# Beginning and end of the MLP of a two-layer encoder trunk: the order of up blocks, Strassen combinations, transposes and weight splits

## The chip, the cores and the metric

The kernel runs on one core of a Trainium2 chip. The time is that of one execution on the device in microseconds (us); of several runs the median is taken. Engines are named as in the profile: PE is TensorE (matrix products and transposes), DVE is VectorE, ACT is ScalarE, POOL is GpSimd, SP is SyncE, which issues the transfers from HBM.

## What is computed

The reference is a trunk of two layers on 512 tokens with 1024 features, in float32. Each layer has a mixer (dilated window attention in layer 0, latent attention in layer 1), a squared-ReLU MLP and a gated input embedding; the change lies in the last two and at their seams:

```
x = x + sq_relu_mlp(rmsnorm(x, mlp_norm[i]), w_up[i], w_down[i])
gate = jax.nn.sigmoid(rmsnorm(x, ple_norm[i]) @ w_ple_gate[i])
x = x + gate * (p[i] @ w_ple_proj[i])
...
def sq_relu_mlp(h, w_up, w_down):
    return jnp.square(jax.nn.relu(h @ w_up)) @ w_down
```

`w_up` is 1024 x 4096, `w_down` 4096 x 1024. The root mean square of `rmsnorm` runs over the 1024 features of a token.

## The kernel before, in words

**Products in three parts.** Every float32 matrix product is made of three products in a reduced type: each operand is split into a rounded high part and the low rest, and `mm3` (lines 219 to 221) adds high x high, low x high (or the mirrored pair) and high x low in one PSUM bank. A weight block of 128 x 1024 comes by DMA into a tile `wr`, ScalarE casts it to the high part `wh` (line 191), VectorE subtracts to get the low part `wl` (line 192). These three tags have three buffers each. Operands made in the kernel are split the same way by `split` (lines 226, 227, with a gain 229, 230) into `unit` tiles `u` of 128 x 1024, of which there are 24; there are 18 `half` tiles `h` of 128 x 512 and 8 PSUM banks `ps`.

**The order of weights** is a list made ahead (`_mlp_blocks`); `load` fetches a block and up to `ahead` (2) of its successors in that list, so its order sets SP's queue. The order of instructions on each engine is settled by a scheduler when the kernel is built, from the order in which the program asks for them; an engine then runs its own list in order and waits for others by semaphores.

**The MLP** (`mlp`, lines 699 to 856) runs over 4 chunks of 1024 hidden features. A chunk has 8 up blocks (`up`: `dense` products into a bank, `relu` on VectorE in line 728, the square on ScalarE in line 730, then the splits of the operands). From the fourth up block on `left` (lines 755 to 765) makes sums and differences of the operand's quarters. The product with `w_down` is a Strassen form with seven products, `prod(c, p)` for p = 1 to 7, each in two halves b = 0, 1 of 12 matrix products; its weights are quarters of `w_down` or their combinations. For these, `quarters` (line 148) issues three loads of 256 KB for each k = 0 to 3 into `half` tiles, and `combine` (lines 153 to 155) makes three differences of each on VectorE. Products share accumulating pairs of banks: P1, P6, P7, P4 follow each other in one pair, P5 and P3 in another, and behind a product `put` adds the banks to `acc` in SBUF (line 719) or copies them (line 722). The seven products of chunk c are interleaved with the up blocks of chunk c + 1; the first chunk's up blocks run ahead of the loop. In layer 0 they begin with `first`, four blocks whose products lie beside the attention's end, then up block 4, the norm's column sums (`columns`: products with ones in line 314, then `rsqrt`, a chain of 13 small VectorE steps in lines 246 to 259) and `row`, which spreads the result over partitions by PE transposes (line 267) and multiplies it in at each `relu`.

**The end of the MLP.** In the last chunk the products run in the order `LAST`; `embed` (lines 858 to 869) makes the embedding's projection of four blocks behind P6 and P7. `turned(m)` transposes a 128-feature block of `acc` back (four PE transposes, line 781), adds it to the residual x (line 341), splits it for the gate's products (lines 229, 230) and squares it for the gate's norm `nG` (ScalarE in lines 288 and 291; the sum of squares in line 292 on `eng`, GpSimd by default, the last of the eight on VectorE). Four of the eight `turned` stand behind P5, ahead of P3, four behind P3. Then `gate` (layer 0) or, in layer 1, a last stage with token halves runs its products with the norm's chain beside gate block 0.

## Time and profile before

| | |
|---|---|
| median of 3 runs | 1255.61 us (1255.6 to 1255.73) |
| the profiled execution's own time | 1254.16 us |
| its span on the core | 1252.3 us |
| mean granted PE clock | 0.991 of full speed |
| PE busy | 1215.8 us, 97% |
| VectorE busy | 972.4 us, 78% |
| ScalarE busy | 673.4 us, 54% |
| GpSimd busy | 136.4 us, 11% |

The profile records one execution: the span runs from the first instruction to the last, and the execution's own time holds 1.9 us around it. Busy time is the time in which an engine works on an instruction; a wait in the timeline stands in brackets in front of the instruction that waited, with the instruction that released it. The granted clock is given as a share of full speed; half speed is the lower of its two levels.

### The profile page before, as it was taken

The numbers are of one execution on the slowest core, as the hardware profiler recorded it, in microseconds if no ns is written. First come the engines' busy times: TensorE is split into PE (matmuls) and PEld (weight loads), VectorE is DVE, ScalarE is ACT, GpSimd is POOL, SyncE is SP. The second block draws the span as 40 slices with busy tenths as digits, with TensorE's granted clock in tenths as the row PEclk, the third lists the DMA queues.
The fourth block names the chain that finished last, engine by engine and source line by source line (L and its number), as shares of the span: only waits on it lengthen the run. The fifth ranks groups of instructions, "written<-read, shape, count | busy, mean of one in ns | idle before, by whom it ended". The sixth has DMA issues, their size and how long they took to land.

```text
span 1252.3 us, 16676 instructions
## 1 busy us (share of the span) xinstructions
PE 1215.8 (97%) x6096; PEld 1028.0 (82%) x6096; DVE 972.4 (78%) x1610; ACT 673.4 (54%) x1111; POOL 136.4 (11%) x177
## 2 busy tenths in 40 slices
PE   8999999999999999999989999999999999999996
PEld 6888878877888888887879888888888888888796
DVE  6566666788777877788878998968777778778877
ACT  5466564564354443555558887754545435435553
POOL 5000000000000000003234443220000000000300
PEclk9999999999999999999999999999999999999998
DMA  6222113263533534422211010126244354343242
GB/s 214 83 68 68 59 51 110 97 214 118 185 126 110 170 123 130 140 101 89 81 51 38 20 49 18 52 84 227 101 150 158 113 185 132 101 142 113 93 152 102
DMA packets 48178, 138.39 MB, mean 111 GB/s; under 512 B 5600, under 2 KB 6368, under 8 KB 48096
## 3 DMA queue, kind: packets, MB, share of 16 engines
q1 hardware_dynamic: 48096, 137.32, 33.2%
q8 instruction: 48, 0.79, 0.3%
q14 instruction: 34, 0.28, 0.1%
HBM read 135.21 MB, written 2.10 MB: 110 GB/s over the span
## 4 chain that ended last, share of the span: by engine, by line
PE 85%; DVE 8%; ACT 5%; issue 1%; DMA 0%; DVEq 0%; SPq 0%; ACTq 0%
PE ps L219 26%; PE ps L221 26%; PE ps L220 26%; PE ps L1057 2%; DVE wl L192 1%; DVE u L227 1%; PE ps L1079 1%; PE ps L1073 1%; DVE u L230 1%; ACT wh L191 1%; ACT u L226 1%; ACT h L226 1%; DVE x L341 1%; ACT qk L440 0%; PE ps L314 0%
## 5 line engine op out<-in xcount | busy, mean ns | idle before, releaser
L191 ACT CAST wh<-wr 128x1024 fp32r<-128x1024 f32 (+4 forms) x197 | 198.2, 1008 | 304.5 <-PE ps L221 235.0
L219 PE MATMUL ps<-wh,u 128*128 128x512 f32 (+4 forms) x720 | 277.2, 387 | 6.3 <-ACT wh L191 5.7
L219 PE MATMUL ps<-u,wh 128*128 128x512 f32 (+1 forms) x744 | 278.6, 374 | 2.4 <-ACT u L229 2.4
L220 PE MATMUL ps<-u,wl 128*128 128x512 f32 (+1 forms) x744 | 277.6, 373 | 3.3 <-DVE wl L192 3.3
L221 PE MATMUL ps<-u,wh 128*128 128x512 f32 (+1 forms) x744 | 276.9, 373 | 0.3 <-DVE u L230 0.3
L220 PE MATMUL ps<-wh,u 128*128 128x512 f32 (+4 forms) x720 | 274.3, 382 | 0.0
L221 PE MATMUL ps<-wl,u 128*128 128x512 f32 (+4 forms) x720 | 273.0, 382 | 0.3 <-DVE wl L192 0.3
L192 DVE TENSOR_TENSOR wl<-wr,wh 128x1024 fp32r<-128x1024 f32 (+4 forms) x197 | 233.3, 1185 | 47.9 <-ACT wh L191 46.6
L220 PEld LDWEIGHTS ps<-u,wl 128*128 128x128 f32 x744 | 141.0, 189 | 28.4 <-DVE wl L192 4.6
L219 PEld LDWEIGHTS ps<-u,wh 128*128 128x128 f32 x744 | 141.3, 190 | 27.2 <-ACT u L229 3.0
L221 PEld LDWEIGHTS ps<-u,wh 128*128 128x128 f32 x744 | 141.0, 189 | 24.8 <-DVE u L230 0.7
L219 PEld LDWEIGHTS ps<-wh,u 128*128 128x128 f32 x720 | 136.1, 189 | 30.0 <-ACT wh L191 6.1
L221 PEld LDWEIGHTS ps<-wl,u 128*128 128x128 f32 x720 | 135.9, 189 | 25.2 <-DVE wl L192 1.3
L220 PEld LDWEIGHTS ps<-wh,u 128*128 128x128 f32 x720 | 136.3, 189 | 23.3 <-DVE u L230 0.3
L292 POOL TENSOR_TENSOR h<-h,h 128x512 f32<-128x512 f32 x24 | 37.5, 1565 | 760.2 <-ACT h L291 759.6
L227 DVE TENSOR_TENSOR u<-ps,u 128x512 fp32r<-128x512 f32 (+4 forms) x148 | 96.5, 666 | 16.1 <-ACT u L226 14.2
L226 ACT CAST u<-ps 128x512 fp32r<-128x512 f32 (+3 forms) x148 | 81.6, 571 | 29.6 <-PE ps L567 11.6
L728 DVE SCALAR_TENSOR_TENSOR u<-ps,h 128x512 f32<-128x512 f32 x64 | 43.5, 688 | 57.9 <-PE ps L221 57.9
L226 ACT CAST wh<-h 128x512 fp32r<-128x512 f32 x96 | 55.3, 619 | 52.3 <-PE ps L220 39.7
L227 DVE TENSOR_TENSOR u<-u,u 128x1024 fp32r<-128x1024 f32 (+1 forms) x66 | 70.9, 1093 | 8.7 <-ACT u L226 8.7
L227 DVE TENSOR_TENSOR wl<-h,wh 128x512 fp32r<-128x512 f32 x96 | 62.2, 688 | 15.4 <-ACT wh L226 15.4
L719 DVE TENSOR_TENSOR acc<-acc,ps 128x512 f32<-128x512 f32 x96 | 63.7, 682 | 4.6 <-PE ps L221 4.5
(177 smaller groups left out, 1685.8 us busy)
## 6 DMA issues: line engine op xcount, KB each, us to landing
wr<-wts SPq DMA_DIRECT2D x182, 512.0 KB, 3.4
h<-wts SPq DMA_DIRECT2D x96, 256.0 KB, 3.7
wr<-wts SPq DMA_DIRECT2D x12, 384.0 KB, 3.1
wr<-wts SPq DMA_DIRECT2D x12, 256.0 KB, 5.1
x<-xT SPq DMA_DIRECT2D x8, 256.0 KB, 6.0
wr<-wts SPq DMA_DIRECT2D x4, 416.0 KB, 3.0
out<-u SPq DMA_DIRECT2D x6, 256.0 KB, 2.2
u<-pT SPq DMA_DIRECT2D x2, 512.0 KB, 4.6
```

What stands on the lines that cost most here:

```text
L191: A.copy(hi[:, c], raw[:, c])
L192: V.tensor_tensor(lo[:, c], raw[:, c], fl(hi[:, c]), op=ALU.subtract)
L219: T.matmul(out_, l[0], r[0], start=first, stop=False, skip_group_check=more)
L220: T.matmul(out_, l[1], r[0], start=False, stop=False, skip_group_check=more)
L221: T.matmul(out_, l[0], r[1], start=False, stop=last, skip_group_check=more)
L226: a = A.copy(hi, src)
L227: v = V.tensor_tensor(lo, src, fl(hi), op=ALU.subtract)
L230: v = V.scalar_tensor_tensor(lo, src, gain, fl(hi), op0=ALU.mult, op1=ALU.subtract)
L292: (V if self.n == KD - 1 else self.eng).tensor_tensor(self.acc, self.acc, sq, op=ALU.add)
L719: V.tensor_tensor(a, a, ps, op=ALU.add)
L728: V.scalar_tensor_tensor(o_, in_(ps), 0.0, in_(rb[0]), op0=ALU.max, op1=ALU.mult)
L1057: T.transpose(pt[:, tok(c)], e[:, tok(c)], ident)
```

## The change

It touches six things. `NEXT` puts two up blocks behind P1 and one behind each later product, in place of one behind each and two at the end. At the beginning of layer 0 the 12 loads of `quarters` are issued right behind up block 4, ahead of `nM.row()`, and the `combine` steps follow the up blocks 3, 5 and 6; in layer 1 the loads move from behind up block 5 to behind 2. The projection's weights and those of the last chunk's P3 are split into `unit` tiles, not into the three-buffer tags, and loaded earlier (behind P1 and ahead of P5). The first four `turned` run between the halves of P5. And `nG` adds its squares on VectorE. Line numbers behind the diff's first insertions are larger by 1 to 19: helpers by 5 (192 is now 197, 292 is 297, 719 is 724, 781 is 786).

```diff
--- before.py
+++ after.py
@@ -42,6 +42,7 @@
 
 PRODUCTS = (1, 2, 6, 5, 7, 3, 4)
 LAST = (1, 2, 6, 7, 4, 5, 3)
+NEXT = (0, 2, 3, 4, 5, 6, 7, 8)
 
 
 def _schedule():
@@ -71,7 +72,7 @@
         for n, p in enumerate(PRODUCTS if c + 1 < NCH else LAST):
             out += [(("prod", l, c, p, b), 0) for b in range(2)]
             if c + 1 < NCH:
-                out += [(("up", l, c + 1, m), 1024) for m in range(n, n + 1 if n < 6 else 8)]
+                out += [(("up", l, c + 1, m), 1024) for m in range(NEXT[n], NEXT[n + 1])]
             elif p == 6:
                 out += [(("proj", l, 0), 1024)]
     out += [(("proj", l, 1), 1024)]
@@ -181,8 +182,12 @@
 
         o, n = offs[key[:3] if key[0] == "gate" else key]
         raw = wp.tile([P, 1024], F32, tag="wr", name=nm("wr"))
-        hi = wp.tile([P, 1024], F32R, tag="wh", name=nm("wh"))
-        lo = wp.tile([P, 1024], F32R, tag="wl", name=nm("wl"))
+        if key[0] == "proj" or key[0] == "quarter" and key[2:4] == (NCH - 1, 3):
+
+            hi, lo = unit(F32R), unit(F32R)
+        else:
+            hi = wp.tile([P, 1024], F32R, tag="wh", name=nm("wh"))
+            lo = wp.tile([P, 1024], F32R, tag="wl", name=nm("wl"))
         src = wts[o:o + P * n].rearrange("(p n) -> p n", n=n)
         fetched[key] = (hi, lo)
         for i in range(pieces):
@@ -782,13 +787,13 @@
             residual(m, pt)
             nG.tile(m)
 
-        def prod(c, p):
+        def prod(c, p, ahead=2, mid=()):
             g = {1: "a", 2: "b", 6: "a", 5: "c", 7: "a", 3: "c", 4: "a"}[p]
             new = p in (1, 2, 5)
             if new:
                 chain[g] = [bank(), bank()]
             for b in range(2):
-                w = load(("prod", l, c, p, b))
+                w = load(("prod", l, c, p, b), ahead)
                 for i in range(2):
                     for k in (2 * b, 2 * b + 1):
                         cs = slice(k % 2 * S, (k % 2 + 1) * S)
@@ -797,14 +802,20 @@
                         for r, n in {1: ((0, 0),), 2: ((0, 0),), 6: ((0, 1),), 5: ((1, 1),), 7: ((1, 1),),
                                      3: ((0, 1),), 4: ((1, 0),)}[p]:
                             put(r, i, n, chain[g][i])
-
-        nG = Norm(G_PLE + 8 * l)
+                for m in mid if b == 0 else ():
+                    turned(m)
+
+        nG = Norm(G_PLE + 8 * l, V)
         if first:
             nM.columns()
             ps = dense(("up", l, 0, 4), KD, nM.k)
+            for k in range(4):
+                quarters(l, 0, k)
             rb[0] = nM.row()
             for m in range(4):
                 up(0, m, first[m])
+            for k in range(2):
+                combine(l, 0, k)
             up(0, 4, ps)
         else:
             ps = [dense(("up", l, 0, 0), KD, nM.k)]
@@ -815,14 +826,18 @@
                 up(0, m, ps[m])
             for m in range(2, 5):
                 up(0, m)
+                if m == 2:
+                    for k in range(4):
+                        quarters(l, 0, k)
+            for k in range(2):
+                combine(l, 0, k)
         for m in range(5, 8):
             up(0, m)
-            if m == 5:
-                for k in range(4):
-                    quarters(l, 0, k)
+            if m < 7:
+                combine(l, 0, m - 3)
         emb, pe = [], []
         for c in range(NCH):
-            for k in range(2):
+            for k in range(2 if c else 0):
                 combine(l, c, k)
             if c == NCH - 1:
                 preload(AF.Sigmoid)
@@ -831,22 +846,26 @@
                 pe += unit(F32R), unit(F32R)
                 split(*pe, pr)
             for n, p in enumerate(PRODUCTS if c + 1 < NCH else LAST):
-                prod(c, p)
-                if n < 2 and (n == 0 or c + 1 < NCH):
+                end = c == NCH - 1
+                if end and p == 5:
+                    for b in range(2):
+                        load(("prod", l, c, 3, b), 0)
+                prod(c, p, 1 if end and p == 3 else 2, range(4) if end and p == 5 else ())
+                if end and p == 1:
+                    for h in range(2):
+                        load(("proj", l, h), 0)
+                if c and n < 2 and (n == 0 or c + 1 < NCH):
                     for k in range(n + 2, n + 3 if c + 1 < NCH else 4):
                         combine(l, c, k)
                 if c + 1 < NCH:
                     if p == 4:
                         for k in range(4):
                             quarters(l, c + 1, k)
-                    for m in range(n, n + 1 if n < 6 else 8):
+                    for m in range(NEXT[n], NEXT[n + 1]):
                         up(c + 1, m)
                 elif p in (6, 7):
                     for m in range(2):
                         embed(l, emb, 2 * (p - 6) + m, *pe)
-                elif p == 5:
-                    for m in range(4):
-                        turned(m)
 
         embed(l, emb, 4, *pe)
         for m in range(4, KD):
```

VectorE at the beginning of layer 0: in both lists the norm's chain (`sm`, 13 steps), the `wl` are weight differences, the `h` steps with lines 154 to 156 are `combine`. Before:

```order
L192 TENSOR_TENSOR wl_2436<-wr_2434,wh_2435 128x1024
L246 TENSOR_SCALAR sm_2473<-ps_2468 128x4
L247 TENSOR_SCALAR sm_2474<-sm_2473 128x4
L248 TENSOR_SCALAR sm_2475<-sm_2473 128x4
L249 TENSOR_SCALAR sm_2475<-sm_2475 128x4
L257 TENSOR_TENSOR sm_2480<-sm_2475 128x4
L258 TENSOR_TENSOR sm_2480<-sm_2480,sm_2474 128x4
L259 SCALAR_TENSOR_TENSOR sm_2481<-sm_2480,sm_2475 128x4
L192 TENSOR_TENSOR wl_2546<-wr_2544,wh_2545 128x1024
L257 TENSOR_TENSOR sm_2485<-sm_2481 128x4
L258 TENSOR_TENSOR sm_2485<-sm_2485,sm_2474 128x4
```

Now, from the same weight difference on; six more `combine` steps stand among the nine small steps that follow, and then the first `relu`:

```order
L197 TENSOR_TENSOR wl_2436<-wr_2434,wh_2435 128x1024
L154 TENSOR_TENSOR h_2520<-h_2521,h_2520 128x512
L155 TENSOR_TENSOR h_2521<-h_2522,h_2521 128x512
L156 TENSOR_TENSOR h_2522<-h_2522,h_2520 128x512
L154 TENSOR_TENSOR h_2526<-h_2527,h_2526 128x512
L155 TENSOR_TENSOR h_2527<-h_2528,h_2527 128x512
L251 TENSOR_SCALAR sm_2473<-ps_2468 128x4
L156 TENSOR_TENSOR h_2528<-h_2528,h_2526 128x512
L252 TENSOR_SCALAR sm_2474<-sm_2473 128x4
L253 TENSOR_SCALAR sm_2475<-sm_2473 128x4
L197 TENSOR_TENSOR wl_2576<-wr_2574,wh_2575 128x1024
L254 TENSOR_SCALAR sm_2475<-sm_2475 128x4
```

The `combine` steps, which stood behind the `relu` steps, stand ahead of the norm's chain and between its steps.

VectorE at the end of layer 0: `acc` are the puts, `x` the residuals, `u` the splits (line 230, now 235), `h` additions of squares (now line 297). Before, with P5's put first and the first bank of P3's last:

```order
L719 TENSOR_TENSOR acc_2465<-acc_2465,ps_4812 128x512
L719 TENSOR_TENSOR acc_2466<-acc_2466,ps_4813 128x512
L341 TENSOR_TENSOR x_76<-x_76,ps_4852 128x512
L341 TENSOR_TENSOR x_76<-x_76,ps_4863 128x512
L341 TENSOR_TENSOR x_77<-x_77,ps_4874 128x512
L230 SCALAR_TENSOR_TENSOR u_4859<-x_76,gains,u_4858 128x512 x2
L341 TENSOR_TENSOR x_77<-x_77,ps_4887 128x512
L230 SCALAR_TENSOR_TENSOR u_4881<-x_77,gains,u_4880 128x512
L192 TENSOR_TENSOR wl_4900<-wr_4898,wh_4899 128x1024
L230 SCALAR_TENSOR_TENSOR u_4881<-x_77,gains,u_4880 128x512
L192 TENSOR_TENSOR wl_4918<-wr_4916,wh_4917 128x1024
L719 TENSOR_TENSOR acc_2464<-acc_2464,ps_4812 128x512
```

Now, with P5's put in the rows of `ps_4830` and `ps_4831` that write `acc_2465` and `acc_2466`:

```order
L346 TENSOR_TENSOR x_76<-x_76,ps_4844 128x512
L346 TENSOR_TENSOR x_76<-x_76,ps_4855 128x512
L346 TENSOR_TENSOR x_77<-x_77,ps_4866 128x512
L235 SCALAR_TENSOR_TENSOR u_4851<-x_76,gains,u_4850 128x512 x2
L297 TENSOR_TENSOR h_2467<-h_2467,h_4863 128x512
L235 SCALAR_TENSOR_TENSOR u_4873<-x_77,gains,u_4872 128x512
L297 TENSOR_TENSOR h_2467<-h_2467,h_4876 128x512
L346 TENSOR_TENSOR x_77<-x_77,ps_4879 128x512
L724 TENSOR_TENSOR acc_2465<-acc_2465,ps_4830 128x512
L724 TENSOR_TENSOR acc_2466<-acc_2466,ps_4831 128x512
L235 SCALAR_TENSOR_TENSOR u_4873<-x_77,gains,u_4872 128x512
L297 TENSOR_TENSOR h_2467<-h_2467,h_4887 128x512
```

The first four residuals and their splits moved ahead of P5's put, the additions of squares stand among them, and the weight differences of the projection are gone from here.

VectorE at the norm of the gate in layer 1 (`sm` is its chain, `h_8075` the sum of squares, `wl` weight differences of gate blocks). Before:

```order
L292 TENSOR_TENSOR h_8075<-h_8075,h_10740 128x512
L246 TENSOR_SCALAR sm_10800<-ps_10795 128x4
L247 TENSOR_SCALAR sm_10801<-sm_10800 128x4
L248 TENSOR_SCALAR sm_10802<-sm_10800 128x4
L249 TENSOR_SCALAR sm_10802<-sm_10802 128x4
L192 TENSOR_TENSOR wl_10824<-wr_10822,wh_10823 128x1024
L257 TENSOR_TENSOR sm_10807<-sm_10802 128x4
L192 TENSOR_TENSOR wl_10869<-wr_10867,wh_10868 128x1024
L258 TENSOR_TENSOR sm_10807<-sm_10807,sm_10801 128x4
```

Now:

```order
L297 TENSOR_TENSOR h_8075<-h_8075,h_10740 128x512
L251 TENSOR_SCALAR sm_10800<-ps_10795 128x4
L252 TENSOR_SCALAR sm_10801<-sm_10800 128x4
L253 TENSOR_SCALAR sm_10802<-sm_10800 128x4
L254 TENSOR_SCALAR sm_10802<-sm_10802 128x4
L197 TENSOR_TENSOR wl_10869<-wr_10867,wh_10868 128x1024
L262 TENSOR_TENSOR sm_10807<-sm_10802 128x4
L263 TENSOR_TENSOR sm_10807<-sm_10807,sm_10801 128x4
L264 SCALAR_TENSOR_TENSOR sm_10808<-sm_10807,sm_10802 128x4
```

One weight difference is left in the chain's beginning; the one that stood before the chain's last step stands behind it.

## Rows read from the trace of the kernel before

**Rows 1.** The page's part 1: busy us (share of the span) xinstructions, by engine.

```profile
PE 1215.8 (97%) x6096; PEld 1028.0 (82%) x6096; DVE 972.4 (78%) x1610; ACT 673.4 (54%) x1111; POOL 136.4 (11%) x177
```

**Rows 2.** PE's timeline: start us, us, what [idle before <-releaser].

```profile
283.19 0.50 PE L220 MATMUL ps<-u,wl 128*128 128x512 f32 x1 [2.13 <-DVE wl L192]
...
569.50 0.50 PE L220 MATMUL ps<-u,wl 128*128 128x512 f32 x1 [0.59 <-DVE wl L192]
...
572.93 0.66 PE L781 MATMUL ps<-ident,acc 128*128 128x128 f32 x4 [2.00 <-DVE acc L719]
...
1175.82 0.50 PE L220 MATMUL ps<-u,wl 128*128 128x512 f32 x1 [0.56 <-DVE wl L192]
...
1179.25 1.12 PE L781 MATMUL ps<-ident,acc 128*128 128x128 f32 x4 [2.01 <-DVE acc L719]
...
1189.91 1.02 PE L314 MATMUL ps<-ones,h 128*128 128x1 f32 x8 [0.23 <-DVE h L292]
...
1196.57 1.09 PE L267 MATMUL ps<-ident,sm 128*128 128x128 f32 x4 [2.66 <-DVE sm L259]
```

**Rows 3.** Windows: length, busy (x) of PE, PEld, DVE, ACT, POOL; PEclk; DMA share; GB/s.

```profile
284.00:289.00 5.00, 5.00 (x16) 3.94 (x15) 5.00 (x6) 1.77 (x2) 0.00 (x0) 0.66 0.67 210
1179.25:1183.00 3.75, 3.75 (x18) 3.54 (x19) 3.21 (x5) 0.81 (x2) 0.00 (x0) 0.58 0.69 213
1196.57:1200.00 3.43, 3.43 (x18) 3.43 (x19) 0.99 (x2) 1.22 (x2) 0.00 (x0) 0.58 0.75 245
```

**Rows 4.** VectorE's timeline, crowd before the wait at 283.19.

```profile
279.58 0.68 DVE L155 TENSOR_TENSOR h<-h,h 128x512 f32<-128x512 f32 x1
280.19 1.22 DVE L227 TENSOR_TENSOR u<-u,u 128x1024 fp32r<-128x1024 f32 x1
```

**Rows 5.** VectorE's timeline, layer 0, before and in the norm's chain.

```profile
239.24 1.23 DVE L192 TENSOR_TENSOR wl<-wr,wh 128x1024 fp32r<-128x1024 f32 x1 [0.99 <-ACT wh L191]
...
252.05 0.16 DVE L246 TENSOR_SCALAR sm<-ps 128x4 f32<-128x4 f32 x1 [3.87 <-PE ps L314]
...
253.19 1.23 DVE L192 TENSOR_TENSOR wl<-wr,wh 128x1024 fp32r<-128x1024 f32 x1
254.33 0.16 DVE L257 TENSOR_TENSOR sm<-sm 128x4 f32<-128x4 f32 x1
...
255.32 0.16 DVE L259 SCALAR_TENSOR_TENSOR sm<-sm,sm 128x4 f32<-128x4 f32 x1
```

**Rows 6.** PE's timeline at the spread of that norm.

```profile
257.23 0.39 PE L221 MATMUL ps<-u,wh 128*128 128x512 f32 x1
257.45 0.60 PE L267 MATMUL ps<-ident,sm 128*128 128x128 f32 x4
```

**Rows 7.** SyncE's queue: issue of the quarters' loads, layer 0.

```profile
254.87 8.05 SPq L148 DMA_DIRECT2D h<-wts  x12
```

**Rows 8.** The page's part 6: issue xcount, KB each, median us to landing.

```profile
h<-wts SPq DMA_DIRECT2D x96, 256.0 KB, 3.7
```

**Rows 9.** Timeline of VectorE and GpSimd, end of layer 0.

```profile
563.91 1.57 DVE L230 SCALAR_TENSOR_TENSOR u<-x,gains,u 128x512 fp32r<-128x512 f32 x2
...
565.36 5.24 POOL L292 TENSOR_TENSOR h<-h,h 128x512 f32<-128x512 f32 x3 [358.41 <-ACT h L291]
...
567.13 2.32 DVE L192 TENSOR_TENSOR wl<-wr,wh 128x1024 fp32r<-128x1024 f32 x1
...
576.32 2.45 DVE L230 SCALAR_TENSOR_TENSOR u<-x,gains,u 128x512 fp32r<-128x512 f32 x2
...
579.29 2.89 DVE L230 SCALAR_TENSOR_TENSOR u<-x,gains,u 128x512 fp32r<-128x512 f32 x2
```

**Rows 10.** VectorE's timeline, the gate norm's chain of layer 1, steps four and five.

```profile
1191.44 0.17 DVE L249 TENSOR_SCALAR sm<-sm 128x4 int32<-128x4 int32 x1
1191.52 1.23 DVE L192 TENSOR_TENSOR wl<-wr,wh 128x1024 fp32r<-128x1024 f32 x1
1192.67 0.16 DVE L257 TENSOR_TENSOR sm<-sm 128x4 f32<-128x4 f32 x1
```


## The prediction

> **What bounds the kernel now.** The page's busy line comes first [rows 1]: TensorE (PE) is busy 1215.8 of 1252.3 us, VectorE (DVE) 972.4, ScalarE 673.4, GpSimd (POOL) 136.4. A change that leaves every matrix product in place can win at most the 36.5 us in which PE is idle, and the time lost where its clock is low. So the second view was PE's timeline, read for bracketed idle times at the places that the diff touches: the beginning of the MLP in layer 0, its four chunks, and its end in both layers. Seven such waits are there [rows 2], all released by VectorE; inside the chunks (288 to 556 and 890 to 1160) and at the beginning in layer 1 none stands. The third view was the granted clock behind each wait [rows 3]: after three of the four waits of 2 us or more PE went on at the lower level (1.2 GHz instead of 2.4, half speed); after the one at 572.93 it did not.
>
> **What can go: waits.** The beginning of layer 0 has 2.13 us, the end of layer 0 0.59 + 2.00 = 2.59, the end of layer 1 0.56 + 2.01 + 0.23 + 2.66 = 5.46; together 10.18 us [rows 2].
>
> **What can go: clock.** In a window in which PE is busy throughout, the share missing from full clock is lost work [rows 3]: 5.00 x (1 - 0.66) = 1.70 us at 284, 3.75 x 0.42 = 1.57 at 1179, 3.43 x 0.42 = 1.44 at 1196. Together 4.71 us, so at most 14.9 us can come back.
>
> **Layer-0 beginning.** The wait at 283.19 is for the low part of an up block (line 192): VectorE had the chain `left`, the last `combine` and two weight differences in its queue. The diff moves the 12 loads of `quarters` and all four `combine` ahead, out of that crowd. A wide step of `combine` holds VectorE 0.61 us (279.58 to 280.19 [rows 4]); 12 of them, 7.3 us, are gone from there, three times the 2.13 us, and one more up block between products gives the low part more room. I count the wait and its 1.70 us of clock as gone.
>
> But they land somewhere. In the new order five combine steps stand ahead of the rsqrt chain of the norm (lines 246 to 259) and seven more, with one weight difference, inside it. The 13 small steps run now from 252.05 to 255.48 with one weight difference (1.14 us, 253.19 to 254.33) among them [rows 5]; PE reaches the transposes that spread the result (line 267) at 257.45 [rows 6], 2 us later, without a wait. The five in front cost nothing if the data is there: the DVE idled 3.87 us just before 252.05 [rows 5], and 5 x 0.61 = 3.05. The seven inside cost 7 x 0.61 = 4.3 us: 255.48 + 4.3 = 259.8. PE then **waits 2.3 to 2.6 us** at the spread, since those transposes stand in its queue in front of the next up block; I take 2.5. Bounds: 0 (the steps of the chain slip into gaps between the wide ones) and 5 (the loads are late: their queue, SP, needs 8.05 us to issue 12 [rows 7]; issued from about 241, behind the weight load whose buffer the difference that ends at 240.5 sets free [rows 5], the last goes out at 249 and lands 3.7 us later by the median [rows 8], 253; every us later than its turn in the chain adds one). A wait of this size took the clock down in three of four cases, so I count **1.70 us of clock** again (bounds 0 and 1.70). The queue's other loads pass to behind these 12; the block that PE needs next was issued ahead of them, the one after is not due for 5 us.
>
> **Chunks.** One up block per product moves one place earlier; the products, their operands and the weight loads stay. PE has no wait there now, and more room for `left` is worth nothing. 0; if the earlier block took space for units from the operands, something could be lost: bounds 0 and +1.
>
> **Ends, what is removed.** In each layer the first four `turned` go ahead of the second half of P5, P3 runs behind, and the proj and P3 weights are split early into units. The waits at 569.50 and 1175.82 (proj's low part) and at 572.93 and 1179.25 (transposes waiting for P3's put) [rows 2] go: the low parts are split right after P1, and P3's put now has nothing on VectorE in front of it but two weight differences whose casts have the 5.4 us of P3 for themselves; its first bank is complete 6 products (1.4 us) before the transposes of that half. Bound: 0.5 us left over in each layer.
>
> **Ends, the new wait.** P3 adds into the banks of P5, so it may begin only when P5's put (line 719) has read them. In the new order that put stands on VectorE behind four residuals, three splits and two squares' additions, 9 steps of 0.61 to 0.75 us, some 5.9 us from the first transpose on; PE in that time does the transposes, 12 products of P5 and 6 of `embed`, 1.9 + 2.7 + 1.4 = 6.0 (0.23 us a product of 512 columns, 257.23 to 257.45 [rows 6]). The put itself is 0.6 us per bank, and its release follows: **about 1.2 us of wait** in each layer, bounds 0 and 2.5.
>
> **Ends, squares from GpSimd to VectorE.** Six additions per layer, about 0.61 us each of VectorE: 3.7 us more work per end. What it takes away: while POOL adds (three in 5.24 us [rows 9]), VectorE's own steps run long. The weight difference at 567.13 took 2.32 us against 1.23 otherwise [rows 5, 9], pairs of splits 2.45 and 2.89 against 1.57 [rows 9]: 1.09 + 0.88 + 1.32 = 3.3 us at one end, and the neighbours not listed make it about 4. I take the two as cancelling. The Trainium skill (Perfetto Trace Analysis, Optimizing Scalar/DVE Operations) says that work may be handed from a saturated VectorE to GpSimd, and warns that the two share an SBUF read port, so that it might not help; by the first half the move back costs 3.7 us an end, by the warning nothing, and the rows side with the warning.
>
> **End of layer 1, the gate's norm.** The chain that releases the spread at 1196.57 carries three weight differences (two behind its fourth and fifth step, one before the last); in the new order one is left. From its fourth step at 1191.44 to the fifth at 1192.67, with one difference between, it took 1.23 us [rows 10] where small steps follow each other at 0.2 (252.05 to 255.32 is 3.27 with 12 distances and one difference [rows 5]), so it ends 2 x 1.0 us sooner; the ones-products (line 314) stand four products of 256 columns later on PE, 0.5 us less work to cover it. Of the 2.66 us **1.1** stay (bounds 0 and 2.66). Gate 0's last block needs the last split, which now has the copies and additions of four tiles in front: **0.5** (bounds 0 and 1). With waits of 1.2 and 1.1 instead of 2.0 and 2.7 I count both clock falls of layer 1 as gone (bound: both stay, 3.0).
>
> **Sum.** Gone: 10.18 + 4.71 = 14.9. New: 2.5 + 1.7 at the beginning, 1.2 at the end of layer 0, 1.2 + 0.5 + 1.1 at the end of layer 1, 8.2. Net -6.7: 1254.16 (the profiled execution's own time) becomes 1247.5. The median of the runs is 1255.61, 1.45 above that execution, so the forecast for the median is **1248.9 us**.
>
> **Rivals**, all as medians:
> 1. *The spread does not wait long*, or its wait leaves the clock up. For: the clock stayed up after 572.93, and loads and steps in front may leave fewer inside. 1.7 to 4.2 us less: 1244.7 to 1247.2. Chance 0.2 (beside 0.5 for the forecast).
> 2. *The shorter waits at the ends still take the clock down.* For: 0.56 + 2.01 sufficed in layer 1, and the new waits also come in pairs. Up to 3.0 more in layer 1 and 1.6 in layer 0: 1251 to 1253.5. Chance 0.17.
> 3. *Slower: VectorE becomes the bound of both ends.* If VectorE's long steps under POOL's additions were waiting for something else anyway, nothing is won back and six additions of 0.61 us lie in front of P5's put and the last splits. Then both ends are 3.7 us later: -6.7 + 7.4 = +0.7, 1256.3, and waits of 4 to 5 us there take the clock down at both, some 4.6 us: +5.3, 1260.9. It decides where P3 waits over 3.5 us. The Trainium skill's advice (same page and section) to offload a saturated engine points this way. Against: VectorE is busy 78% and its stretched rows coincide with POOL's. Chance 0.08.
> 4. *The change does nothing measurable*: the new waits (up to 5 at the spread, 2.5 at each P3, 2.66 at the norm) eat what went: 5 + 1.7 + 2 x 2.5 + 2.66 = 14.4 against 14.9, 1255.1. Chance 0.05.
>
> **How the numbers follow.** A measurement of this kernel tells about 0.2%, 2.5 us, from no change: faster means under 1253.1, slower over 1258.1. Forecast and rival 1 are faster, and most of rival 2: 0.5 + 0.2 + 0.11 = 0.81. Within: the rest of rival 2, rival 4 and part of rival 3: 0.13. Slower 0.06. The range goes from 1245, by the good end of rival 1, to 1254, past rival 2; outside lie rival 3, most of rival 4 and a little below.
>
> **What would show it.** In the profile of the changed kernel: no wait of PE for an up block's low part near 280; a wait of 2 to 3 us at the spread near 257, released by VectorE's last chain step, with combine steps between the small ones; no wait at the second transposes; a wait of about 1 us at P3's first product, released by the put; at the gate's norm of layer 1 about 1.1 us; no POOL additions at the ends, and VectorE's splits back at 0.75 us. The forecast is wrong if the spread does not wait, if P3 waits over 3 us, or if a new wait opens inside the chunks.

## The result and the profile after

The changed kernel takes **1243.47 us** (median of 4 executions, 1242.67 to 1243.79) where the kernel before took 1255.61 beside it (1254.02 to 1255.73): a ratio of 0.9905, 95% interval 0.9888 to 0.9922. The profiled execution's own time is 1243.45 us, its span 1241.7, its mean granted clock 0.995 where before it was 0.991. The forecast was 1248.9, its range 1245 to 1254: the direction was right, the gain larger than the range allowed, by 1.5 us beyond its good end.

The page's busy line of the changed kernel stands against [rows 1]:

```profile
PE 1211.3 (98%) x6096; PEld 1023.5 (82%) x6096; DVE 967.8 (78%) x1622; ACT 672.9 (54%) x1111; POOL 116.7 (9%) x165
```

PE is idle 30.4 us of the span in place of 36.5, VectorE works 4.6 us less in spite of 12 more additions (for the most part not because of them, see e6), and GpSimd 19.7 us less. PE's timeline of the changed kernel has these waits at the places of [rows 2] (start, length, what, idle time before and releaser):

```profile
258.75 0.65 PE L272 MATMUL ps<-ident,sm 128*128 128x128 f32 x4 [1.39 <-DVE sm L264]
...
562.98 0.50 PE L224 MATMUL ps<-u,u 128*128 128x512 f32 x1 [1.12 <-DVE acc L724]
...
1166.84 0.50 PE L224 MATMUL ps<-u,u 128*128 128x512 f32 x1 [1.11 <-DVE acc L724]
...
1181.81 0.38 PE L226 MATMUL ps<-u,wh 128*128 128x256 f32 x1 [0.29 <-DVE u L235]
...
1187.14 0.62 PE L272 MATMUL ps<-ident,sm 128*128 128x128 f32 x4 [1.11 <-DVE sm L264]
```

The seven waits of 10.18 us are gone, and five new ones of 5.02 us are there: the spread of the norm in layer 0 (the transposes that spread its result over the partitions, 1.39), P3 behind P5's put in both layers (1.12 and 1.11), the last split for gate 0 (0.29) and the spread of the gate's norm (1.11). In the windows behind the four larger ones (length, busy time of PE, PEld, DVE, ACT and POOL, granted clock, DMA share, GB/s) the clock is at its upper level throughout, where two of [rows 3] stood at 0.58 and one at 0.66:

```profile
258.70:263.00 4.30, 4.25 (x21) 3.60 (x22) 2.43 (x3) 2.89 (x4) 0.00 (x0) 1.00 0.50 148
563.00:568.00 5.00, 5.00 (x22) 4.11 (x23) 4.62 (x6) 0.62 (x2) 0.00 (x0) 1.00 0.22 71
1166.80:1171.00 4.20, 4.16 (x18) 3.48 (x19) 4.12 (x5) 0.69 (x2) 0.00 (x0) 1.00 0.03 8
1187.20:1191.00 3.80, 3.80 (x33) 3.80 (x34) 3.06 (x5) 1.51 (x3) 0.00 (x0) 1.00 0.55 216
```

How far each place moved, from the same waits and products in both traces: at the end of layer 0 (the column sums of the next norm, 631.17 before, 626.86 now) the kernel is 4.31 us ahead, at the wait of 0.29 behind the latent attention's first products (748.61 and 743.34) 5.27, at the spread of the last norm (1245.81 and 1235.14) 10.67. So layer 0 gave 4.31, of which 0.28 was there before the change begins (223.50 and 223.22); the attention of layer 1, which the change does not touch, gave 0.96; the MLP of layer 1, its end that is, gave 5.40. The lines, of before and then of the changed kernel:

```profile
631.17 1.05 PE L314 MATMUL ps<-ones,h 128*128 128x1 f32 x8 [0.44 <-DVE h L292]
...
748.61 0.50 PE L220 MATMUL ps<-u,u 128*128 128x512 f32 x1 [0.28 <-DVE u L227]
...
1245.81 0.69 PE L267 MATMUL ps<-ident,sm 128*128 128x128 f32 x2 [2.47 <-DVE sm L259]
```

```profile
626.86 1.05 PE L319 MATMUL ps<-ones,h 128*128 128x1 f32 x8 [0.44 <-DVE h L297]
...
743.34 0.50 PE L225 MATMUL ps<-u,u 128*128 128x512 f32 x1 [0.29 <-DVE u L232]
...
1235.14 0.69 PE L272 MATMUL ps<-ident,sm 128*128 128x128 f32 x2 [2.47 <-DVE sm L264]
```

The chain that now sets the spread in layer 0, on VectorE, to be read against [rows 5]; its first step, a stretch from its middle and its end:

```profile
251.79 0.16 DVE L251 TENSOR_SCALAR sm<-ps 128x4 f32<-128x4 f32 x1 [0.48 <-PE ps L319]
...
254.41 0.16 DVE L262 TENSOR_TENSOR sm<-sm 128x4 f32<-128x4 f32 x1
254.59 0.69 DVE L155 TENSOR_TENSOR h<-h,h 128x512 f32<-128x512 f32 x1
255.20 0.15 DVE L263 TENSOR_TENSOR sm<-sm,sm 128x4 f32<-128x4 f32 x1
255.27 0.69 DVE L154 TENSOR_TENSOR h<-h,h 128x512 f32<-128x512 f32 x1
...
258.14 0.16 DVE L262 TENSOR_TENSOR sm<-sm 128x4 f32<-128x4 f32 x1
258.34 0.16 DVE L263 TENSOR_TENSOR sm<-sm,sm 128x4 f32<-128x4 f32 x1
258.54 0.16 DVE L264 SCALAR_TENSOR_TENSOR sm<-sm,sm 128x4 f32<-128x4 f32 x1
```

A small step (`sm`) starts about 0.60 us behind the start of the wide one in front of it, and the next wide one 0.07 to 0.18 us behind the small one's start: a pair takes 0.67 to 0.79 us. Alone, small steps follow each other at 0.20. That distance belongs to steps that need the result of the step in front: the second and third step of this chain, which both need only the first one's result, start 0.07 apart (252.47 and 252.54). So a wide step that depends on neither fills the time in which the next small one would have waited for its operand.

### The profile page after: what moved, and what is told of

It is laid out like the page before. It is cut to its first block, busy times and chain, and to the rows that moved or that the text cites. A ratio compares the mean times of both kernels' runs of the same rounds, so it can differ in the third digit from the quotient of the medians.

```text
span 1241.7 us, 16628 instructions
## 1 busy us (share of the span) xinstructions
PE 1211.3 (98%) x6096; PEld 1023.5 (82%) x6096; DVE 967.8 (78%) x1622; ACT 672.9 (54%) x1111; POOL 116.7 (9%) x165
## 4 chain that ended last, share of the span: by engine, by line
PE 85%; DVE 8%; ACT 6%; issue 1%; DMA 0%; DVEq 0%; SPq 0%; ACTq 0%
PE ps L224 26%; PE ps L226 26%; PE ps L225 26%; PE ps L1076 2%; DVE u L232 1%; ACT u L231 1%; PE ps L1098 1%; PE ps L1092 1%; DVE wl L197 1%; ACT u L234 1%; ACT wh L196 1%; DVE x L346 1%; ACT h L231 1%; ACT h L1062 1%; DVE sm L1061 1%
## 5 line engine op out<-in xcount | busy, mean ns | idle before, releaser
L196 ACT CAST wh<-wr 128x1024 fp32r<-128x1024 f32 (+4 forms) x189 | 190.0, 1007 | 317.8 <-PE ps L226 228.5
L224 PE MATMUL ps<-wh,u 128*128 128x512 f32 (+4 forms) x704 | 270.4, 386 | 6.3 <-ACT wh L196 5.7
L225 PE MATMUL ps<-wh,u 128*128 128x512 f32 (+4 forms) x704 | 267.5, 381 | 0.0
L224 PE MATMUL ps<-u,wh 128*128 128x512 f32 (+1 forms) x712 | 264.9, 372 | 2.4 <-ACT u L234 2.4
L226 PE MATMUL ps<-wl,u 128*128 128x512 f32 (+4 forms) x704 | 266.8, 382 | 0.4 <-DVE wl L197 0.4
L226 PE MATMUL ps<-u,wh 128*128 128x512 f32 (+1 forms) x712 | 263.8, 371 | 0.3 <-DVE u L235 0.3
L225 PE MATMUL ps<-u,wl 128*128 128x512 f32 (+1 forms) x712 | 263.8, 370 | 0.0
L197 DVE TENSOR_TENSOR wl<-wr,wh 128x1024 fp32r<-128x1024 f32 (+4 forms) x189 | 221.1, 1172 | 46.5 <-ACT wh L196 45.3
L224 PEld LDWEIGHTS ps<-wh,u 128*128 128x128 f32 x704 | 132.8, 189 | 29.1 <-ACT wh L196 5.9
L224 PEld LDWEIGHTS ps<-u,wh 128*128 128x128 f32 x712 | 134.3, 189 | 25.7 <-ACT u L234 3.2
L226 PEld LDWEIGHTS ps<-u,wh 128*128 128x128 f32 x712 | 134.2, 189 | 23.8 <-DVE u L235 1.0
L225 PEld LDWEIGHTS ps<-u,wl 128*128 128x128 f32 x712 | 134.4, 189 | 22.8
L225 PEld LDWEIGHTS ps<-wh,u 128*128 128x128 f32 x704 | 133.0, 189 | 22.7 <-DVE u L235 0.3
L231 ACT CAST u<-u 128x1024 fp32r<-128x1024 f32 (+1 forms) x66 | 60.9, 947 | 13.9 <-DVE u L767 12.9
```

What stands on the lines that cost most here:

```text
L196: A.copy(hi[:, c], raw[:, c])
L197: V.tensor_tensor(lo[:, c], raw[:, c], fl(hi[:, c]), op=ALU.subtract)
L224: T.matmul(out_, l[0], r[0], start=first, stop=False, skip_group_check=more)
L225: T.matmul(out_, l[1], r[0], start=False, stop=False, skip_group_check=more)
L226: T.matmul(out_, l[0], r[1], start=False, stop=last, skip_group_check=more)
L231: a = A.copy(hi, src)
```

## The experiments

Every median below is of 4 to 10 executions. "Before" stands for the executions of the kernel before on the same chip at the same time.

### How steady the times are: e1 and e5

e1 is the kernel before and e5 the changed kernel, both without an edit.

> The kernel before, unchanged. What is asked: three executions took 1255.6 us and two 1254.1, and the prediction carried the 1.45 us between them over to the changed kernel. Theory: the longer executions have one more fall of TensorE's clock (some 1.5 us), so their mean granted clock is about 0.990 where the profiled one has 0.991, and the changed kernel, with fewer waits that can take the clock down, has no such pair. Rival: the 1.45 us lie outside the span or in transfers, and the clocks of all executions are alike.

> The changed kernel, unchanged, as the base for the three beside it. The kernel before ran between 1252.1 and 1257.3 us in 24 executions, with mean granted clocks of 0.988 to 0.994; the first four executions of the changed kernel lay between 1242.7 and 1243.8 with 0.995 and 0.996. Theory: its waits of 1.1 to 1.4 us take the clock down seldom, so it stays near 1243.5 with a small spread. Rival: the four were lucky, and executions of 1245 to 1248 turn up.

Measured: e1 1254.2 us, 1252.46 to 1257.28, beside 1253.99 (1252.1 to 1255.06), ratio 1.0005 (0.9996 to 1.0015). In all, 49 executions of the kernel before lie between 1252.1 and 1258.4, with medians of 1253.6 to 1254.3 in three sessions; the three 1255.6 with which it was shown were at the upper side. The two fastest of e1's session, 1252.1 and 1252.27, have a mean clock of 0.993, those of 1254.48 and 1254.55 have 0.989 and 0.988; but the two slowest of e1, 1257.1 and 1257.28, have 0.989 and 0.99. The clock makes part of these differences, not all of them. e5: 1243.59 us, ratio 0.9924 (0.9908 to 0.9941); of eight executions of the changed kernel seven lie between 1242.67 and 1243.79, one at 1245.4 with a clock of 0.993. So the change is worth **about 10 us** on these chips, and the 12 of the first comparison hold 1.5 us of that session's kernel before.

### The beginning of layer 0: e2, e3, e4

e2 puts the loads and the combine steps of the first chunk back, in layer 1 too (those lines are not shown):

```diff
-            for k in range(4):
-                quarters(l, 0, k)
             rb[0] = nM.row()
...
-            for k in range(2):
-                combine(l, 0, k)
             up(0, 4, ps)
...
         for m in range(5, 8):
             up(0, m)
-            if m < 7:
-                combine(l, 0, m - 3)
+            if m == 5:
+                for k in range(4):
+                    quarters(l, 0, k)
...
-            for k in range(2 if c else 0):
+            for k in range(2):
                 combine(l, c, k)
...
-                if c and n < 2 and (n == 0 or c + 1 < NCH):
+                if n < 2 and (n == 0 or c + 1 < NCH):
```

> The changed kernel with the quarters' loads and the combine steps of the first chunk back where they were before, in both layers. Theory: the wait of 1.39 us at the spread of the norm goes; a wait for an up block's low part comes back near 280, 2.1 us or less, with a clock fall of 1.7 if it is as long as before: between 1242.1 and 1246. Rival (the new order of up blocks, NEXT, had already removed that wait): no wait near 280, 1242.1.

Measured: 1247.15 us (ratio 0.9948, 0.9931 to 0.9965), 3.6 above e5 and 1.1 above the range that I gave. The spread does not wait, as expected. The wait near 280 is back, longer than before (2.63 us in place of 2.13, so the new order of up blocks did not shorten it), and the clock falls behind it; the profile is of the fastest of four executions, 1245.28, and what the slower ones lost beyond this is not shown:

```profile
281.96 0.51 PE L225 MATMUL ps<-u,wl 128*128 128x512 f32 x1 [2.63 <-DVE wl L197]
```

```profile
281.00:286.00 5.00, 4.04 (x11) 3.18 (x12) 5.00 (x6) 2.67 (x3) 0.00 (x0) 0.66 0.50 172
```

e3 takes the old order of up blocks:

```diff
-NEXT = (0, 2, 3, 4, 5, 6, 7, 8)
+NEXT = (0, 1, 2, 3, 4, 5, 6, 8)
```

> The changed kernel with one up block behind each product and two at the end again. Theory: with the combine steps moved away the low part is in time also in the old order, no wait inside the chunks, 1243.5 within 0.5. Rival: NEXT was needed, a wait of 1 to 2 us near 280 and a clock fall of 1.7: 1244.5 to 1247.3.

Measured: 1243.4 us (0.9919, 0.9904 to 0.9933), no wait near 280, the waits of the changed kernel elsewhere. The new order of up blocks gives nothing that can be seen; with e2 it is shown that moving the loads and the combine steps does all of it at this place.

e4 puts more of the combine steps inside the norm's chain, by holding them behind its first step (`held`, taken in `rsqrt`):

```diff
+            held = tail[0].ins
...
+            with tc.issue_after(held):
+                for k in range(4):
+                    combine(l, 0, k)
...
-            if m < 7:
+            if m < 7 and not first:
```

> The changed kernel with all first-chunk combine steps of layer 0 behind the first step of the norm's chain, so that eleven wide steps stand inside the chain in place of seven and one weight difference. Theory: a small step beside a wide one costs 0.07 us and not 0.20, so the chain ends at 251.8 + 11 x 0.67 + 0.6 = 259.8, and PE waits 2.5 us at the spread in place of 1.39. If a wait of that length takes the clock down, as three of four did before, the time is 1243.5 + 1.1 + 1.7 = 1246.3; rival, that the place decides and not the length: the clock stays up, 1244.6.

Measured: 1246.08 us (0.9932, 0.9917 to 0.9947). The chain, now with eleven wide steps and no weight difference inside, runs from 252.00 to 259.66, 7.66 us: with each wide step added in full it would be 3.43 - 1.14 + 11 x 0.61 = 9.0, and by pairs its end had been expected at 259.8. The spread waits 2.15 us, less than the 2.5 expected, and the clock falls behind it for 5.00 x 0.34 = 1.70 us of work:

```profile
259.72 0.65 PE L274 MATMUL ps<-ident,sm 128*128 128x128 f32 x4 [2.15 <-DVE sm L266]
```

```profile
260.00:265.00 5.00, 5.00 (x18) 3.98 (x17) 3.74 (x5) 1.95 (x4) 0.00 (x0) 0.66 0.60 217
```

Three of its four executions took 1246.04 to 1246.44 us (clock 0.992 to 0.994), the fourth 1242.98 with 0.996. So a wait of 2.15 us at this place costs its own length and a clock fall (one profile shows it; the time and the mean clock say the same of three executions in four). The wait of 1.39 us left the clock up in both profiles of the changed kernel, and in those of e3, e6, e7 and e8, which have it too.

### The squares and the turned tiles: e6, e7, e9

e6 gives the additions of squares back to GpSimd:

```diff
-        nG = Norm(G_PLE + 8 * l, V)
+        nG = Norm(G_PLE + 8 * l)
```

> The changed kernel with the six additions of squares per layer back on GpSimd. The prediction took the additions on VectorE (3.7 us an end) and the stretch of VectorE's steps beside GpSimd as cancelling. Theory: so it is for the sum, the stretched steps stand partly in front of P5's put, whose two additions in front are gone; P3's waits stay within 0.7 of 1.1 us, the time within 1.5 of the changed kernel's. Rival one (GpSimd's additions really hold up VectorE): waits of P3 and of the gate's norm grow by 2 us or more at each end, and clock falls follow, 1246 to 1251. Rival two (work handed to GpSimd is work saved): P3's waits vanish, 1241.5.

Measured: 1244.68 us (0.9926, 0.9911 to 0.994), 1.1 above e5 and within the interval of it. P3's waits shrink to 0.38 and 0.35, a little more than the 0.7 us that I allowed, as two additions fewer stand in front of P5's put, and the spread of the gate's norm does not wait; yet the clock falls there:

```profile
562.57 0.50 PE L224 MATMUL ps<-u,u 128*128 128x512 f32 x1 [0.38 <-DVE acc L724]
...
1167.65 0.50 PE L224 MATMUL ps<-u,u 128*128 128x512 f32 x1 [0.35 <-DVE acc L724]
...
1182.80 0.38 PE L226 MATMUL ps<-u,wh 128*128 128x256 f32 x1 [0.36 <-DVE u L235]
...
1183.49 1.02 PE L319 MATMUL ps<-ones,h 128*128 128x1 f32 x8 [0.31 <-DVE h L297]
```

```profile
1185.00:1190.00 5.00, 5.00 (x31) 5.00 (x31) 2.81 (x12) 1.21 (x2) 0.00 (x0) 0.66 0.31 105
```

Three of its four executions have a clock of 0.992 (1244.39 to 1245.49), the fourth 0.996 (1242.61). Here waits of 0.36 and 0.31 us within a microsecond went ahead of the fall; what decides it is not the length of a wait alone.

This run also prices the squares by themselves. VectorE is busy 967.4 us in it, 967.8 and 968.0 in the two profiles of the changed kernel: 12 additions more, and only 0.4 to 0.6 us. The additions (line 297) take 22.6 us in place of 14.3; the splits with a gain take 35.9 in place of 42.2 and the weight differences 0.8 less. The splits of e6, then of the changed kernel (count, busy us, mean ns, and the idle time before them):

```profile
L235 DVE SCALAR_TENSOR_TENSOR u<-x,gains,u 128x512 fp32r<-128x512 f32 x48 | 42.2, 883 | 15.9 <-ACT u L234 15.4
```

```profile
L235 DVE SCALAR_TENSOR_TENSOR u<-x,gains,u 128x512 fp32r<-128x512 f32 x48 | 35.9, 750 | 17.8 <-ACT u L234 17.5
```

e7 puts the first four turned tiles behind P5 again:

```diff
-                prod(c, p, 1 if end and p == 3 else 2, range(4) if end and p == 5 else ())
+                prod(c, p, 1 if end and p == 3 else 2)
...
+                elif p == 5:
+                    for m in range(4):
+                        turned(m)
```

> The changed kernel with the first four transposed tiles behind P5 again and P3's weights still split early into units. Theory: P3 does not wait for P5's put, which the transposes cover; VectorE has eight tiles' residuals, splits and additions from then on, about 2 us a tile of which P3 and an embedding product cover 6.8 us, so the second transposes wait 1 to 2 us again in each layer: 1243.5 to 1245.5 without clock falls, up to 3 more with them. Rival (the early units alone had freed VectorE): no wait for the second transposes, 1241.3.

Measured: 1242.22 us (0.9911, 0.9896 to 0.9925), 1.4 faster than e5, with one of four executions as slow as those of e5 (1243.59): the rival of this run was nearer than the theory. P3 does not wait, and neither do the second transposes; at the end of layer 1 gate 0 waits for the last split's high part, on ScalarE:

```profile
1179.94 0.38 PE L224 MATMUL ps<-u,wh 128*128 128x256 f32 x1 [0.87 <-ACT u L234]
...
1180.72 0.39 PE L226 MATMUL ps<-u,wh 128*128 128x256 f32 x1 [0.28 <-DVE u L235]
...
1185.98 0.62 PE L272 MATMUL ps<-ident,sm 128*128 128x128 f32 x4 [1.11 <-DVE sm L264]
```

So running the first four transposed tiles inside P5 costs here: it brings two waits of 1.1 us at P3 and saves one of 0.87.

e9 is the kernel before with the early units alone:

```diff
+        if key[0] == "proj" or key[0] == "quarter" and key[2:4] == (NCH - 1, 3):
+            hi, lo = unit(F32R), unit(F32R)
...
+                if end and p == 5:
+                    for b in range(2):
+                        load(("prod", l, c, 3, b), 0)
...
+                if end and p == 1:
+                    for h in range(2):
+                        load(("proj", l, h), 0)
```

> The kernel before with nothing but the early loads and early splits of the projection's and P3's weights into units. Taking the units away from the changed kernel alone cost 13 us. Theory: the units carry most of the ends: the waits for the projection's low part (0.59, 0.56) go, and the second transposes wait less than half of the 2.0 us, since two weight differences are out of P3's put's way; the rest at the end of layer 1 (about 2.5 us at the spread of the gate's norm) and the 2.1 us near 280 with its clock fall stay: 1253.9 - 1.15 - 2.0 to 4.0 and the clock fall of 1.6 in layer 1 = 1247.5 to 1251. Rival (the units only undo the harm that the new order at the ends does): 1252.5 to 1254.

Measured: 1248.84 us beside 1254.26 (0.9953, 0.9935 to 0.9972), 5.4 us better than before and within the range expected, by two misses that make up for each other: of 2.66 us at the gate's norm, which I had expected to stay, 0.64 are left, and the second transposes still wait 1.7 us, where I had expected less than half of 2.0. The projection's waits are gone:

```profile
571.30 0.33 PE L786 MATMUL ps<-ident,acc 128*128 128x128 f32 x1 [1.74 <-DVE acc L724]
...
1176.10 0.33 PE L786 MATMUL ps<-ident,acc 128*128 128x128 f32 x1 [1.71 <-DVE acc L724]
...
1190.33 0.62 PE L272 MATMUL ps<-ident,sm 128*128 128x128 f32 x4 [0.64 <-DVE sm L264]
```

The ends of e7 and e9 differ in the engine of the squares alone (the up blocks and the combine steps, in which they differ too, lie elsewhere). On VectorE, steps on the way to P3's put, in e9 and then in e7:

```profile
566.64 2.31 DVE L197 TENSOR_TENSOR wl<-wr,wh 128x1024 fp32r<-128x1024 f32 x1
568.88 1.76 DVE L235 SCALAR_TENSOR_TENSOR u<-x,gains,u 128x512 fp32r<-128x512 f32 x1
570.57 1.27 DVE L724 TENSOR_TENSOR acc<-acc,ps 128x512 f32<-128x512 f32 x2
```

```profile
565.74 1.22 DVE L197 TENSOR_TENSOR wl<-wr,wh 128x1024 fp32r<-128x1024 f32 x1
566.87 0.74 DVE L235 SCALAR_TENSOR_TENSOR u<-x,gains,u 128x512 fp32r<-128x512 f32 x1
...
568.13 0.68 DVE L724 TENSOR_TENSOR acc<-acc,ps 128x512 f32<-128x512 f32 x1
```

Beside GpSimd's additions the weight difference takes 2.31 us and the split 1.76, without them 1.22 and 0.74. With the tiles behind P5, the squares on VectorE are what removes the second transposes' wait of 1.7 us. In the changed kernel, with the tiles inside P5, their place hardly matters (e6). The transposes inside P5 and the squares on VectorE are two cures for one wait, and with the squares on VectorE the transposes inside P5 leave only their price.

One thing more can be read from these profiles. From the wait behind the latent attention's first products to the spread of the last norm, the whole of layer 1's MLP, the kernel before takes 497.20 us, e9 491.82 (746.46 to 1238.28), the changed kernel 491.80 and e7 491.16. In layer 1 the early units alone give what the whole change gives, since most of what the squares on VectorE remove at the second transposes comes back at the gate. The profile of e9 is of its fastest execution (1246.59), so the other three may have lost more here.

### The weights in units: e8

e8 is the changed kernel with these weights in the three-buffer tags again, loaded at their old places:

```diff
-        if key[0] == "proj" or key[0] == "quarter" and key[2:4] == (NCH - 1, 3):
-            hi, lo = unit(F32R), unit(F32R)
-        else:
-            hi = wp.tile([P, 1024], F32R, tag="wh", name=nm("wh"))
-            lo = wp.tile([P, 1024], F32R, tag="wl", name=nm("wl"))
+        hi = wp.tile([P, 1024], F32R, tag="wh", name=nm("wh"))
+        lo = wp.tile([P, 1024], F32R, tag="wl", name=nm("wl"))
...
-                if end and p == 5:
-                    for b in range(2):
-                        load(("prod", l, c, 3, b), 0)
-                prod(c, p, 1 if end and p == 3 else 2, range(4) if end and p == 5 else ())
+                prod(c, p, 2, range(4) if end and p == 5 else ())
...
-                if end and p == 1:
-                    for h in range(2):
-                        load(("proj", l, h), 0)
```

> The changed kernel with the projection's and P3's last weights in the three-buffer tags and loaded at their old places. Theory: the weight differences come back into VectorE's crowd at the end, three of 1.14 us, one in front of P5's put, and the wait for the projection's low part (0.56 to 0.59 before) or for P3's weights returns: 1 to 2.5 us per layer, 1245.5 to 1248.5. Rival (the early split brings nothing): 1243.5 within 0.5.

Measured: 1256.62 us, slower than before (1.0021, 1.0011 to 1.003), and 13.0 above e5. In each layer the projection waits for its high part and then P3 for P5's put, which on VectorE has a weight difference, a split and an addition more in front; from about 563.2 to 570 the clock is at its lower level, and as long in layer 1:

```profile
561.25 0.51 PE L220 MATMUL ps<-u,wh 128*128 128x512 f32 x1 [1.22 <-ACT wh L192]
...
564.90 0.79 PE L220 MATMUL ps<-wh,u 128*128 128x512 f32 x1 [3.15 <-DVE acc L720]
...
1171.87 0.50 PE L220 MATMUL ps<-u,wh 128*128 128x512 f32 x1 [1.21 <-ACT wh L192]
...
1175.53 0.79 PE L220 MATMUL ps<-wh,u 128*128 128x512 f32 x1 [3.16 <-DVE acc L720]
```

```profile
563.00:570.00 7.00, 5.10 (x12) 4.04 (x13) 3.58 (x5) 0.12 (x1) 0.00 (x0) 0.51 0.45 150
1174.00:1181.00 7.00, 5.47 (x13) 4.31 (x14) 3.21 (x5) 0.33 (x1) 0.00 (x0) 0.51 0.48 150
```

The waits make 2 x (1.22 + 3.15 - 1.1) = 6.5 us of the 13.0, and the last split for gate 0 0.5 more (0.80 in place of 0.28); the clock makes most of the rest, (5.10 + 5.47) x 0.49 = 5.2 us of work in these two windows. My expectation fell short of the waits (2.5 us a layer at most, where 3.3 came) and left the clock out.

### Better than both: e10 and e11

e10 holds the combine steps behind the norm's chain (`tail[1]` is its last step) and puts the embedding products of two blocks, not one, between P5 and P3:

```diff
+            held = tail[1].ins
...
+            with tc.issue_after(held):
+                for k in range(4):
+                    combine(l, 0, k)
...
+                elif p == 5:
+                    for m in (4, 5):
+                        embed(l, emb, m, *pe)
...
-        embed(l, emb, 4, *pe)
...
```

> The changed kernel with the combine steps of the first chunk of layer 0 held behind the norm's chain, and two embedding products in place of one between P5 and P3. Theory: the 1.39 us at the spread go, P3's wait of 1.1 us per layer is covered by 1.4 us more of products, the second transposes wait at most 0.5: 1243.6 - 1.4 - 2.2 = 1240.0, up to 1241. Rival: combine behind the chain delays the first relu steps, and the wait comes back at the second chunk's first up block: 1243 to 1245.

Measured: 1241.29 us beside 1254.26 (0.9897, 0.9878 to 0.9915). The spread and both P3 do not wait, nor do the second transposes; gate 0 waits 1.32 us in return (at 1178.59), and in the profile the clock falls behind it (0.50 from 1182 to 1184). The time is just above the 1241 that I gave at most.

e11 holds the combine steps in the same way, with the turned tiles behind P5 as in e7.

> The changed kernel with the first four transposed tiles behind P5 again (1242.2 so far) and the combine steps held behind the norm's chain. Theory: 1242.2 - 1.39 = 1240.8; P3 does not wait, the gate's first block waits about 1.1 us for the last splits. Rival as in the run beside it: no gain from the chain, 1242.2 or more.

Measured: **1240.11 us** beside 1254.26 (0.9885, 0.9868 to 0.9902), 1238.83 to 1241.0, as expected (1240.8): the fastest median of the study, below both kernels. Between 225 us and the next layer's norm PE waits nowhere for 0.2 us or more; at the end of layer 1 these are left:

```profile
1178.61 0.39 PE L224 MATMUL ps<-u,wh 128*128 128x256 f32 x1 [0.88 <-ACT u L234]
...
1179.39 0.39 PE L226 MATMUL ps<-u,wh 128*128 128x256 f32 x1 [0.28 <-DVE u L235]
...
1184.65 0.62 PE L274 MATMUL ps<-ident,sm 128*128 128x128 f32 x4 [1.11 <-DVE sm L266]
```

## Why the prediction was wrong, and where it was right

By its own sum, at the profiled execution's own time: forecast -6.7, measured 1243.45 - 1254.16 = -10.7.

- **What goes.** All seven waits and the three clock falls of [rows 2, 3] went, as counted.
- **The step that failed: the layer-0 beginning, 2.5 + 1.7.** The wait is there, at the place and with the releaser named, with the combine steps between the small ones; but it is 1.39 us. The chain starts at 251.79 and ends at 258.70, 6.9 us, where 3.43 + 7 x 0.61 = 7.7 was counted: each wide step was added to the chain in full, while most small steps beside one cost 0.07 us and not 0.20. That is 0.8 of the 1.1 us between forecast and wait; the rest is a start 0.26 us sooner and the rounding of 259.8 - 257.45 up to 2.5. e4, with its eleven wide steps in 7.66 us, bears out the count by pairs. The second half of the term went with the first: the 1.70 us of clock were counted for a wait "of this size", and at 1.39 us the clock stayed up. In e4, with 2.15 us at the same place, the 1.70 us are there. Together 2.8 us of the 4.0 that were missing.
- **The attention of layer 1, 0.96 us, was not in the sum**, and is not the change's. On VectorE one small step of a norm there falls beside GpSimd's memsets; in the profile of before it took 1.80 us, in that of the changed kernel 0.90, and in e5, the same changed kernel, 1.80 again. With 1.80 PE waits 0.82 us for a ScalarE step behind it (at 652.01 in before), with 0.90 it does not. Of the 13 profiles seven have 1.80 and six 0.90, of kernels with the same attention, so which one comes is chance as far as these runs show. The first, of before, the second of the changed kernel, the third of e5:

```profile
647.96 1.80 DVE L249 TENSOR_SCALAR sm<-sm 128x4 int32<-128x4 int32 x1
```

```profile
643.62 0.90 DVE L254 TENSOR_SCALAR sm<-sm 128x4 int32<-128x4 int32 x1
```

```profile
642.60 1.80 DVE L254 TENSOR_SCALAR sm<-sm 128x4 int32<-128x4 int32 x1
```

- **The ends were right**: P3's wait 1.12 and 1.11 (forecast 1.2), the last split 0.29 (0.5), the spread of the gate's norm 1.11 (1.1), no clock falls in layer 1; the end of layer 1 gave 5.40 (5.67). At P3 the size is part luck. PE is through with its own work 6.0 us behind the first transpose, as counted, but P5's put begins 6.4 us behind it and not 5.9 (555.86 to 562.24), and P3 waits for the put of one bank, 0.6 us, where the forecast needs both to come to 1.2.
- **Squares taken as cancelling**: right. e6 is 1.1 us slower and cannot be told from the changed kernel, and the 12 additions cost VectorE 0.4 to 0.6 us net: nearly all of their work comes back as splits and weight differences that GpSimd no longer stretches. The 4.6 us by which VectorE's busy time fell from before are therefore not theirs; with the early units alone (e9) it is 970.6, 1.8 less than before. The warning that the Trainium skill gives (Perfetto Trace Analysis, Optimizing Scalar/DVE Operations), that handing work from VectorE to GpSimd might not help because they share a read port, agrees with this sum. Its advice to offload a saturated VectorE finds no clear support: with the additions on GpSimd P3 waits 0.7 us less (e6), but where the tiles stand behind P5 the 1.7 us wait stays that e7 does not have (e9). Rival 3, the slower side, did not come: P3 waits 1.12 us, not over 3.5.
- **The other terms put at nothing.** No wait opened inside the chunks, and e3 shows NEXT at nothing, as said.
- **The 1.45 us between profile and median** were added to the forecast as if they belonged to the kernel. They belonged to three executions: over 49, the median of before is about 1254, next to its profiled execution's 1254.16. Without them the forecast had been 1247.5.
- Rival 1 (the spread does not wait long, or its wait leaves the clock up; 1244.7 to 1247.2, chance 0.2) is what happened: 2.8 us less than the forecast is 1246.1. The 1.45 us that were not the kernel's and the 0.96 of the attention, both chance, took it past the range.

What stays open is why the clock falls where it does: 2.00 and 1.98 us before the second transposes of layer 0 left it up in two profiles of the kernel before, and 1.74 and 1.71 in e9; 2.13 and 2.15 near 283 took it down, 1.32 at gate 0 in e10, and in e6 two waits of a third of a microsecond.

## What to carry to other kernels

A wide step put between dependent small steps of the same engine costs less than its length, because it fills the small steps' own wait; work out the pair, not the sum. When a change holds two cures for one wait, test each without the other: here the transposes moved into P5 cost about 1.4 us, because the additions on VectorE, with the early splits, were enough to remove the wait that they were to cover. And look how far a kernel's executions differ before you carry an offset between a profile and a median into a forecast.

## What was not expected of the hardware

A VectorE step of 0.16 us on four columns took 0.90 or 1.80 us beside GpSimd's memsets (8 in 7.26 us, 0.91 each), one or two memsets long, in executions of the same program. That it waits for them is read from the lengths alone; no run moved the memsets. And the ends show how dear the clock is beside the wait that goes with it: in e8 the two falls cost 5.2 us of work, beside 6.5 us by which the waits at the projection and P3 are longer than in the changed kernel.
